# Attention times values: one more output store held back behind the last load, and SyncE's semaphore relays written as a register loop

## The chip, the cores and the metric

One core of one Trainium2 chip. The metric is the device time of one execution in microseconds (us), lower is better; medians of several executions are given. A profiled execution also has a *span*, from its first to its last instruction, which is about 2 us shorter than the device time. "Granted clock" is the share of full TensorE clock in the records. All runs below are of the fast state.

The engines by the names of the profile: PE (TensorE) makes the transposes and the products, DVE (VectorE) and ACT (ScalarE) copy their results, POOL (GpSimd) and SyncE (SP) issue transfers. A transfer is cut into packets, which the core's 16 DMA engines carry; it has *landed* when its semaphore says so.

## The reference

```python
def setup_inputs():
    batch, n_heads, seq, head_dim = 8, 12, 1024, 64
    ...                         # attn_weights (8,12,1024,1024), v (8,12,1024,64), float32
def reference(attn_weights, v):
    return np.einsum('bhqs,bhsd->bhqd', attn_weights, v).astype(np.float32)
```

403 MB of weights are read once, 25 MB of `v` are read and 25 MB of output are written. Heads are taken four at a time, in 24 groups (`NV = 24`); a group has two *units* of weights (`NU = 48`), each 8 MB of float32 in memory that become 4 MB of bfloat16 in SBUF.

## The kernel before: the parts that matter here

POOL issues all loads of weights and `v` and most stores. They stand in one ring, the software queue q0 of the profile. A load may be issued when PE has transposed the buffer that it overwrites. Group 0's `v` comes through SyncE.

```python
HELD = 6
HELD_FROM = NV - 1 - HELD          # 17
BY_SYNC = HELD_FROM + 3            # 20
BY_EIGHTS = HELD_FROM // 2         # 8: groups 0..15 use two output buffers in turn
NO = 2 + NV - 2 * BY_EIGHTS        # later groups have an output buffer each
...
for n in range(NU - 2):            # POOL
    pool.wait_ge(s_t[True], (n + 1) * PER_DVE)      # unit n is transposed
    load_attn(n + 2)
    if n % 2 == 0:
        q = n // 2
        ...                                          # wait for s_sp, then load_v(q + 1)
        if 0 < q <= HELD_FROM:
            store(q - 1)
for q in range(HELD_FROM, BY_SYNC):  # held stores 17, 18, 19: same ring, behind the last load
    store(q)
pool.drain()
```

The two units of the last group are loaded as halves (`s_second` is the second half's semaphore). SyncE passes on landings to the engines ("relays"), straight code for all 48 units. Then it stores groups 20 to 22 through its own ring (q1), then the last group in three pieces, and waits for all landings:

```python
for n in range(-2, NU - 2):
    if n + 2 < HALVED:
        nc.sync.wait_ge(s_abf[n % 2], 16 * ((n + 2) // 2 + 1))
    else:
        nc.sync.wait_ge(s_second[n + 2], 16)
    nc.sync.sem_inc(s_half)
    ...                                # every second n: s_v -> s_vr, landed store -> s_free
for q in range(BY_SYNC, NV - 1):
    store(q, by_sync=True)
...                                    # the last group: 512 KB, then 2 x 256 KB
for q in range(2 * BY_EIGHTS - 2, BY_SYNC):
    nc.sync.wait_ge(s_osb[slot(q)], ...)
nc.sync.wait_ge(s_end, 16 * (NV - 1 - BY_SYNC + 3))
```

Of the kernel before, what the change touches and what calls it, by code (L numbers as in the profile page):

```python
# [10 lines left out]
def kernel(  # L11
# [18 lines left out]
    nc = tc.nc  # L30
# [15 lines left out]
    NV = NH // VH  # L46
    NU = 2 * NV


    HELD = 6  # L50
    HELD_FROM = NV - 1 - HELD
    BY_SYNC = HELD_FROM + 3

    BY_EIGHTS = HELD_FROM // 2
    NO = 2 + NV - 2 * BY_EIGHTS

    HALVED = NU - 2

    def slot(q):
        return q % 2 if q < 2 * BY_EIGHTS else q - 2 * BY_EIGHTS + 2  # L60
# [15 lines left out]
    with tc.tile_critical(no_gpsimd_drain=True):  # L76
# [17 lines left out]
        s_abf = [sem(f"s_abf{i}") for i in range(2)]  # L94
        s_second = {n: sem(f"s_second{n}") for n in range(HALVED, NU)}
        s_v0, s_v = sem("s_v0"), sem("s_v")
        s_osb = [sem(f"s_osb{i}") for i in range(NO)]
# [13 lines left out]
        s_memset, s_const, s_vr = sem("s_memset"), sem("s_const"), sem("s_vr")  # L111

        s_half, s_free = sem("s_half"), sem("s_free")
# [206 lines left out]
        def store(q, by_sync=False):  # L320
            eng = nc.sync if by_sync else pool
            eng.wait_ge(s_out, 2 * q + 3)
            eng.dma_start(  # L323
                out=out_q[q],
                in_=osb[slot(q)].rearrange("p r d -> p (r d)"),
                **({} if by_sync else {"single_packet": True}),
            ).then_inc(s_end if by_sync else s_osb[slot(q)], 16)
# [9 lines left out]
            base=0,  # L337
# [4 lines left out]
        for h in range(VH):  # L342
# [6 lines left out]
                base=0,  # L349
# [3 lines left out]
        for n in range(NU - 2):  # L353
            pool.wait_ge(s_t[True], (n + 1) * PER_DVE)
# [3 lines that stand above are left out]
# [4 lines left out]
                if 0 < q <= HELD_FROM:  # L362
                    store(q - 1)
        for q in range(HELD_FROM, BY_SYNC):
            store(q)
# [2 lines left out]

        nc.sync.dma_start(out=v32.rearrange("p b x -> p (b x)"), in_=v_g[0]).then_inc(s_v0, 16)
        nc.sync.sem_inc(s_free, 2)  # L370
        for n in range(-2, NU - 2):

            if n + 2 < HALVED:
                nc.sync.wait_ge(s_abf[n % 2], 16 * ((n + 2) // 2 + 1))
            else:
                nc.sync.wait_ge(s_second[n + 2], 16)
            nc.sync.sem_inc(s_half)  # L377
            if n >= 0 and n % 2 == 0:
                q = n // 2
                nc.sync.wait_ge(s_v, 16 * (q + 1))  # L380
                nc.sync.sem_inc(s_vr)
                if 0 < q <= 2 * (BY_EIGHTS - 1):
                    nc.sync.wait_ge(s_osb[slot(q - 1)], 16 * ((q - 1) // 2 + 1))
                    nc.sync.sem_inc(s_free)
        for q in range(BY_SYNC, NV - 1):
            store(q, by_sync=True)
        rows = osb[slot(NV - 1)].rearrange("p (u half j) d -> p u half j d", u=2, half=2)
# [3 lines left out]
        for k in range(2):  # L391
            nc.sync.wait_ge(s_fin[k], 1)
            js = ds(4 * k, 4)
            nc.sync.dma_start(out=outs[:, 1, :, js], in_=rows[:, 1, :, js]).then_inc(s_end, 16)
        for q in range(2 * BY_EIGHTS - 2, BY_SYNC):
            nc.sync.wait_ge(s_osb[slot(q)], 16 * BY_EIGHTS if q < 2 * BY_EIGHTS else 16)
        nc.sync.wait_ge(s_end, 16 * (NV - 1 - BY_SYNC + 3))

# [29 lines left out]
```

## Time and profile before

| kernel before | |
|---|---|
| median on record before the change ran | 1055.79 us (1055.35 to 1056.08) |
| span of the profiled execution | 1053.9 us |
| busy share of PE / DVE / ACT | 71% / 37% / 38% |
| DMA engines' time filled by POOL's ring | 99.3% |
| last load landed | 1034.89 us |
| last copies of results done | 1048.54 us |

The reading begins with the row of the DMA engines and not with PE. The prediction shows the lines. One fact is not in any averaged view: the core's 16 DMA engines each have their own sequence of packets, and they do not finish together. So the tail of the run has to be read from the packet records.

### The profile page before, as it was taken

Reading aid. Unit: us, or ns where it says so; the run is one execution under the profiler, and the core shown is the slowest. Engines: PE = TensorE matmul, PEld = TensorE weight load, DVE = VectorE, ACT = ScalarE, POOL = GpSimd, SP = SyncE. Lnnn points to the kernel's source line nnn. Section 1 sums busy time; section 2 is a strip of 40 time slices with the busy share of each in tenths; the row PEclk is TensorE's granted clock in tenths of the full one; section 3 lists DMA queues with packets and bytes.
Section 4 is the critical chain, followed back from the end, with each engine's and each line's share of the span. In section 5 each row is a group of like instructions: output and inputs, shape, how many; then the busy total and the mean of one; then the engine's idle time right before and its main releaser. Section 6 shows DMA issues by size and latency. Waiting matters only on the chain.

```text
span 1053.9 us, 16410 instructions
## 1 busy us (share of the span) xinstructions
PE 752.7 (71%) x6920; PEld 707.1 (67%) x6920; DVE 388.1 (37%) x582; ACT 403.1 (38%) x489; POOL 52.4 (5%) x102
## 2 busy tenths in 40 slices
PE   0976686766878568776686767876678768776895
PEld 0866586756867568676676666765667758776784
DVE  1533343323433234332343333533334334433442
ACT  0543343433444334433353333433334334433452
POOL 1000000000000000000000000000000000000000
PEclk9989888888789888888888888988788898888897
DMA  9999999999999999999999999999999999999998
GB/s 220 219 219 207 239 230 219 238 210 246 238 218 233 209 240 238 218 238 214 243 238 214 236 220 229 238 219 238 234 222 231 219 211 218 218 219 218 211 218 314
DMA packets 14662, 239.67 MB, mean 227 GB/s; under 512 B 1600, under 2 KB 2112, under 8 KB 5184
## 3 DMA queue, kind: packets, MB, share of 16 engines
q0 software_dynamic: 13392, 234.36, 99.3%
q1 hardware_dynamic: 1264, 5.24, 1.2%
q8 instruction: 2, 0.03, 0.0%
q14 instruction: 4, 0.03, 0.0%
HBM read 427.82 MB, written 25.17 MB: 430 GB/s over the span
## 4 chain that ended last, share of the span: by engine, by line
DMA 76%; PE 22%; issue 1%; POOL 0%; DVE 0%; ACT 0%; SPq 0%; POOLq 0%
DMA abf<-in_attn_weights_dram 76%; PE bank L123 22%; PE bank L165 0%; PE bank L150 0%; POOL abf L310 0%; DVE osb L233 0%; ACT ot L262 0%; POOLq L423 0%; SPq L377 0%; SPq L76 0%
## 5 line engine op out<-in xcount | busy, mean ns | idle before, releaser
L123 PE MATMUL bank<-ident,abf 128*128 128x128 f32 x3072 | 468.7, 326 | 262.2 <-DMA abf<-in_attn_weights_dram 255.8
L123 PEld LDWEIGHTS bank<-ident,abf 128*128 128x128 f32 x3072 | 459.2, 215 | 275.1 <-DMA abf<-in_attn_weights_dram 268.3
L250 DVE COPY at<-bank 128x1024 bf16<-128x1024 bf16 x480 | 320.4, 689 | 495.0 <-PE bank L123 491.2
L250 ACT COPY at<-bank 128x1024 bf16<-128x1024 bf16 x288 | 289.1, 1012 | 428.2 <-PE bank L123 428.2
L165 PE MATMUL bank<-at,vbf 128*64 128x256 bf16 x3072 | 215.0, 278 | 0.0
L165 PEld LDWEIGHTS bank<-at,vbf 128*64 128x64 bf16 x3072 | 196.7, 108 | 13.4 <-DVE at L250 4.0
L262 ACT COPY ot<-bank 128x512 f32<-128x512 f32 x48 | 28.1, 585 | 181.1 <-PE bank L165 181.1
L262 DVE COPY ot<-bank 128x512 f32<-128x512 f32 x48 | 33.2, 692 | 151.4 <-PE bank L165 151.4
L150 PE MATMUL bank<-ident,ot 128*128 128x128 f32 x392 | 52.2, 276 | 33.0 <-DVE vbf L226 32.2
L150 PEld LDWEIGHTS bank<-ident,ot 128*128 128x128 f32 x392 | 43.4, 141 | 45.0 <-DVE vbf L226 44.0
L310 POOL DMA_DIRECT2D abf<-in_attn_weights_dram x50 | 26.6, 532 | 896.2 <-PE bank L123 895.2
L233 ACT COPY osb<-bank 128x512 f32<-128x512 f32 x97 | 52.1, 589 | 22.5 <-PE bank L150 22.5
L226 DVE CAST vbf<-bank 128x512 bf16<-128x512 f32 x48 | 30.9, 686 | 6.5 <-PE bank L138 6.5
L226 ACT CAST vbf<-bank 128x512 bf16<-128x512 f32 x48 | 25.8, 589 | 11.9 <-PE bank L138 11.9
L138 PE MATMUL bank<-vr,spread 32*128 32x512 bf16 x384 | 25.7, 377 | 0.0
L138 PEld LDWEIGHTS bank<-vr,spread 32*128 32x128 bf16 x384 | 9.9, 92 | 6.9
L316 POOL DMA_DIRECT2D vr<-in_v_dram x23 | 12.1, 528 | 19.2 <-PE bank L138 18.8
L323 POOL DMA_DIRECT2D out_dram<-osb x20 | 10.7, 537 | 37.3 <-ACT osb L233 37.3
L250 ACT ACT_TABLE_LOAD x8 | 10.3, 1283 | 1.2 <-SPq L76 1.1
L300 DVE CAST vr<-v 128x2048 bf16<-128x2048 f32 x1 | 1.4, 1403 | 3.3 <-DMA v<-in_v_dram 3.3
L344 POOL TENSOR_SCALAR_AFFINE_SELECT spread<-spread 32x512 bf16<-32x512 bf16 x4 | 2.5, 628 | 0.6
L233 DVE COPY osb<-bank 128x512 f32<-128x512 f32 x1 | 0.7, 692 | 3.1 <-PE bank L150 3.1
(8 smaller groups left out, 2.1 us busy)
## 6 DMA issues: line engine op xcount, KB each, us to landing
abf<-in_attn_weights_dram POOLq DMA_DIRECT2D x46, 4096.0 KB, 33.2
out_dram<-osb POOLq DMA_DIRECT2D x20, 1024.0 KB, 34.2
vr<-in_v_dram POOLq DMA_DIRECT2D x23, 512.0 KB, 34.2
abf<-in_attn_weights_dram POOLq DMA_DIRECT2D x4, 2048.0 KB, 25.8
out_dram<-osb SPq DMA_DIRECT2D x3, 1024.0 KB, 11.4
v<-in_v_dram SPq DMA_DIRECT2D x1, 1024.0 KB, 4.9
out_dram<-osb SPq DMA_DIRECT2D x1, 512.0 KB, 7.8
out_dram<-osb SPq DMA_DIRECT2D x2, 256.0 KB, 3.2
```

Source lines behind the costliest of these rows:

```text
L123: last = pe.matmul(out=pt[g % 4][:, k], lhsT=words[:, k], rhs=ident, is_transpose=True, start=(k == 0), stop=(k == KW - 1),)
L138: last = pe.matmul(out=ps, lhsT=spread[rows, b], rhs=vr[rows, b], start=(b == 0), stop=(b == VB - 1),)
L150: last = pe.matmul(out=ps[:, ds(j * P, P)], lhsT=ot[:, j0 + j], rhs=ident, is_transpose=True, start=(j == 0), stop=(j == jn - 1),)
L165: last = pe.matmul(out=outs, lhsT=vbf[:, 2 * kw + par, h], rhs=at[:, ds(half * GH, GH), kw, ds(h * VP, VP), par], start=(n == 0), stop=(n ...
L226: copy(out=vbf[:, :, h], in_=ps.rearrange("p (k d) -> p k d", k=SB)).then_inc(s_vbf[e])
L233: return copy(out=rows.rearrange("p (half j) d -> p j half d", half=2)[:, ds(j0, jn)], in_=ps[:, ds(0, jn * P)].rearrange("p (j half d) -> ...
L250: ins = copy(out=at[:, g].rearrange("c k j two -> c (k j two)"), in_=bank[g % 4].bitcast(bf16),)
L262: copy(out=ot.rearrange("c j (h p) -> c h j p", h=VH)[:, ds(2 * e, 2)], in_=po[e].rearrange("c (h j p) -> c h j p", h=2, j=GH),).then_inc( ...
L310: pool.dma_start(out=abf[n % 2][:, ds(g0, gn)].rearrange("p g s -> p (g s)"), in_=attn_q[n // 2][:, ds((n % 2 * G + g0) * S, gn * S)],).th ...
L316: pool.dma_start(out=vr.rearrange("p b x -> p (b x)"), in_=v_g[iv]).then_inc(s_v, 16)
L323: eng.dma_start(out=out_q[q], in_=osb[slot(q)].rearrange("p r d -> p (r d)"), **({} if by_sync else {"single_packet": True}),).then_inc(s_ ...
L344: pool.affine_select(out=spread[ds(h * VP, VP)], in_=spread[ds(h * VP, VP)], compare_op=mybir.AluOpType.not_equal, fill=1.0, base=0, patte ...
```

## The change

Its intent: hold seven stores instead of six, so that the last load comes earlier by one store, with the additional store in the ring of the loads; and shorten SyncE's instruction stream by a loop over eight heads (two groups) per pass.

```diff
-    HELD = 6
+    HELD = 7
     HELD_FROM = NV - 1 - HELD
-    BY_SYNC = HELD_FROM + 3
+    BY_SYNC = HELD_FROM + 4
...
-        for n in range(-2, NU - 2):
-            ...                     # waits and increments as above, straight
+        def relay(to, of, n):
+            nc.sync.wait_ge(of, n)
+            nc.sync.sem_inc(to)
+        ...
+        with nc.Fori(1, BY_EIGHTS, 1, engines=(mybir.EngineType.SP,)) as it:
+            base = nc.sync.snap(it * 32)
+            stored = nc.sync.snap(it * 16)
+            for k in range(2):
+                relay(s_half, s_abf[0], base + 16 * (k + 1))
+                relay(s_vr, s_v, base + 16 * k)
+                relay(s_free, s_osb[k], stored)
+                relay(s_half, s_abf[1], base + 16 * (k + 1))
+        for q in range(2 * BY_EIGHTS - 1, NV - 1):
+            relays_of(q)            # straight, as before
```

Group 16's store moves from the loop to behind the last load. `BY_EIGHTS` stays 8 and the number of output buffers stays 10.

> **What bounds the kernel now.** I read the page first: its busy shares, its DMA rows and its chain.
>
> ```profile
> PE 752.7 (71%) x6920; PEld 707.1 (67%) x6920; DVE 388.1 (37%) x582; ACT 403.1 (38%) x489; POOL 52.4 (5%) x102
> DMA  9999999999999999999999999999999999999998
> q0 software_dynamic: 13392, 234.36, 99.3%
> q1 hardware_dynamic: 1264, 5.24, 1.2%
> DMA 76%; PE 22%; issue 1%; POOL 0%; DVE 0%; ACT 0%; SPq 0%; POOLq 0%
> ```
>
> No compute engine is above 71%, the DMA engines are full in every slice, and the ring of POOL's transfers (q0) alone fills 99.3% of them. The 22% of PE in the chain are no evidence against that: a load may only be issued when PE has transposed the buffer it overwrites, so the chain runs through both. But a load of 4096 KB takes 33.2 us from issue to landing (the page's median) while one lasts about 20 us, so it stands in the ring some 13 us before the engines reach it. The limit is the sum of the bytes.
>
> Next, the chain in order of time, to see what one store costs inside the loop. The first five lines lie in iterations with a store, the next four without one (the kernel before stores its last one in the iteration at 786 to 829):
>
> ```profile
> 698.19 9.10 PE bank L123 x64
> ...
> 741.74 9.46 PE bank L123 x64
> ...
> 785.30 9.86 PE bank L123 x64
> ...
> 870.05 10.07 PE bank L123 x64
> ...
> 911.14 10.06 PE bank L123 x64
> ...
> 952.58 9.48 PE bank L123 x64
> ...
> 1003.96 30.91 DMA abf<-in_attn_weights_dram
> 1034.89 0.02 SPq L377
> 1034.95 5.75 PE bank L123 x32
> 1047.85 0.69 DVE osb L233
> ```
>
> Two units last 43.55 and 43.56 us with a store, 41.09 and 41.44 without (mean 41.27): a store of 1 MB in the ring costs about 2.3 us. The last load lands at 1034.9, and from there the remaining work on the last unit runs to 1048.5 before its last stores can go.
>
> Last, the stretches of that tail (columns: from:to, length, busy us of PE, PEld, DVE, ACT, POOL, granted clock, DMA share, GB/s):
>
> ```profile
> 1034.90:1038.00 3.10, 3.05 (x14) 3.05 (x15) 0.87 (x2) 1.01 (x1) 0.00 (x0) 0.50 1.01 428
> 1044.00:1046.00 2.00, 1.98 (x30) 1.66 (x27) 0.69 (x1) 0.00 (x0) 0.00 (x0) 1.00 1.02 430
> 1046.00:1048.00 2.00, 1.07 (x8) 0.86 (x8) 0.15 (x1) 1.17 (x2) 0.00 (x0) 1.00 0.95 395
> 1048.00:1049.00 1.00, 0.00 (x0) 0.00 (x0) 0.54 (x1) 0.00 (x0) 0.00 (x0) 1.00 0.40 162
> 1049.00:1050.00 1.00, 0.00 (x0) 0.00 (x0) 0.00 (x0) 0.00 (x0) 0.00 (x0) 0.56 1.01 350
> 1050.00:1051.00 1.00, 0.00 (x0) 0.00 (x0) 0.00 (x0) 0.00 (x0) 0.00 (x0) 0.50 0.62 214
> ```
>
> The six held stores keep the DMA full until about 1047.7. Only then is there a hole, 0.6 us wide on average in one microsecond, before the last unit's stores fill the engines again. That average hides what decides the case. The trace's packet records (start, duration, queue, size) chain end to start into 16 sequences, one for each DMA engine. They end their loads at different times, 1031.7 to 1034.5. The last one then has 24 packets of 8 KB from the ring of the loads and 24 from SyncE's, 0.307 us each (14.7 us, to 1049.3), 8 of 4 KB (1.25 us) and 32 of 1 KB (1.36 us): its last byte is at 1051.9, which is where the sequence does end, without a gap over 0.06 us. The span ends 2.0 us later. The engine that finishes last has no hole to be filled; the hole belongs to the engines that were ahead.
>
> **What the Trainium skill says.** "DMA: Bandwidth & Descriptors", section "Issuing engines are not separate DMA queues": transfers issued by different engines end up on the same 16 DMA engines and interleave. The trace agrees: in the tail both rings are at work and the rate stays at 428 to 430 GB/s, as with one. Its section "Queues, rings and completion order" has each engine take turns between the rings it has work for; so it matters little for the sum in which ring a store stands. Its section "Anatomy of one DMA" gives about 2.0 us of fixed cost, most of it the receipt after the last byte; here 1051.9 to 1053.9 fits. For the loop, "Advanced Engine Details and Errata", section "Control Flow Timing", gives 51 ns for a branch and 108 ns for compare-and-branch.
>
> **The change, part by part.**
> *The store moved.* HELD 6 to 7 moves the store of head group 16 from the loop to behind the last load, in the same ring; BY_SYNC stays 20, so SyncE's three stores are as before, and the number of osb buffers stays 10. Removed ahead of the last load: 8 packets of 8 KB on each DMA engine, 8 x 0.307 = 2.45 us, so the last load should land near 1032.4. Everything computed after it moves forward by as much: the last copies end near 1046.1 instead of 1048.5. Added after it: the same 2.45 us on each engine. For the slowest engine: 1034.5 - 2.45 = 1032.1, plus 56 packets x 0.307 = 17.2, plus 1.25 and 1.36, is 1051.9 again. What was gained before the landing is given back behind it: **0 us**. The engines that are ahead lose their hole of 0.5 to 0.9 us, which does not end the program sooner.
>
> *The relays in a loop.* SyncE waits for landings and raises s_half, s_vr and s_free. The order of these waits per iteration is the same as in the straight code, and the order of the other engines' instructions is unchanged but for the moved store. New is a little register arithmetic and one compare-and-branch for every two head groups, seven passes: with the skill's figure about 0.1 us each, plus the arithmetic. None of it is on the path: PE asks for s_half after half a unit of transposes, some 4 us after the landing of the same load, and SyncE's waits end with the DMA:
>
> ```profile
> SPq L377 <- DMA abf<-in_attn_weights_dram: 938.8, 48, 24.5
> SPq L381 <- DMA vr<-in_v_dram: 57.8, 23, 3.6
> ```
>
> The page's only waits of PE for SyncE (6.2 us) are with the halved loads of the end, which stay outside the loop. **0 us**.
>
> *Instruction words.* Fewer words of SyncE need fetching. In the span of the kernel before four packets of 8 KB of the instruction queue lie between the loads' (at 83, 427, 874 and 921 us), 0.3 us each on one engine; the one at 921 fell on an engine that was among the last. The trace does not tell which sequencer they fed. If one of the slowest engine's goes away, that is -0.3 us; I take about half: **-0.2 us**. If the loop fetched its words anew on each pass it would be plus, but PE runs 23 passes of its loop here and DVE 24, with only these four.
>
> Sum: 1055.8 - 0.2 = **1055.6 us**.
>
> **The rivals.** *The tail has room.* If the six stores ended before the last unit does, a seventh would be free and the gain 2.3 to 2.45 us, to 1053.4. For it: the mean share of 0.40 at 1048 to 1049 and the chain of waits, which ends in PE and DVE and not in the stores. Against it: the slowest engine's unbroken sequence. A part of it can come true if that engine is another one in other runs: with all engines level, the mean hole would be worth about 0.7 us.
> *The fuller ring delays the last stores.* The last unit's stores stand in SyncE's ring behind 3 MB and share the engines with 4 MB instead of 3 in the other. If the engines served the rings unevenly, they would land later, but only into time when the other ring is empty; the sum is the same. Small loss, below 0.5 us.
> *SyncE's loop becomes a wait.* Late relays would have to be over 4 us late to hold PE, and PE then some 10 us to starve the ring. To lose 2% (21 us) each of the seven passes would have to cost 3 us that nothing hides. I see no sign of it.
>
> **Range and chances.** The three runs before lie 0.7 us apart; which DMA engine is last, and by how much, depends on slow packets early in the run, so I allow about half a microsecond for that. Below, room for part of the first rival; above, for the second and some instruction fetches. 8 in 10: 1054.3 to 1056.5. Two per cent are 21 us, ten times more than the whole tail can hold: within 2% is 0.98.
>
> **What would show it.** Right: the chain's last load lands 2.2 to 2.6 us earlier, the last copies end as much earlier, and the stretch from the last load to the end of the span grows by as much (19.0 to about 21.4 us), with the DMA share near 1.0 until about 1049 and no dip to 0.4; SyncE's waits are still for DMA alone; the period of the iterations without a store stays at 41.3 us. Wrong: a span near 1051.5 with the tail still 19 us long (the tail had room, and the unbroken sequence was misread), or waits of PE or ACT for SyncE in the middle of the run, or more instruction packets (the loop costs).

## The result, and the profile after

1055.78 us median (1055.50 to 1056.49, 6 runs); the kernel before in the same rounds 1056.09 us (1055.35 to 1056.88, 6 runs). The ratio is 0.9998, 95% interval 0.9986 to 1.0011: the same. (Ratios are the mean time of one kernel's fast runs over that of the other's of the same rounds, so not quite the ratio of the medians.)

The page of the changed kernel answers with almost the same numbers; POOL's ring line is the same to the last digit. One line that differs is the instruction queue's, three packets instead of four:

```profile
q14 instruction: 3, 0.02, 0.0%
DMA 75%; PE 23%; issue 1%; POOL 0%; DVE 0%; ACT 0%; SPq 0%; POOLq 0%
```

The chain in order of time (start, duration, what). The iteration that lost its store is the one from 785 to 826:

```profile
741.84 10.01 PE bank L123 x64
...
785.40 10.32 PE bank L123 x64
...
826.50 10.29 PE bank L123 x64
...
1032.10 0.02 SPq L374
...
1032.16 6.03 PE bank L123 x32
...
1045.34 0.69 DVE osb L233
```

With its store, that iteration took 43.64 us in the kernel before (785.30 to 828.94); now it takes 41.10. The last load lands at 1032.10 instead of 1034.89, and the last copies are done at 1046.03 instead of 1048.54. Up to here the change gives what it was meant to give, 2.5 to 2.8 us. The span ends at 1053.6 instead of 1053.9. The tail from the last load to the end has grown from 19.0 to 21.5 us. The stretches of the tail (columns as in the prediction) show where the time went:

```profile
1044.00:1046.00 2.00, 1.06 (x8) 0.86 (x8) 0.66 (x1) 0.68 (x2) 0.00 (x0) 1.00 1.04 438
1046.00:1048.00 2.00, 0.00 (x0) 0.00 (x0) 0.04 (x1) 0.00 (x0) 0.00 (x0) 0.74 0.96 398
1048.00:1049.00 1.00, 0.00 (x0) 0.00 (x0) 0.00 (x0) 0.00 (x0) 0.00 (x0) 0.50 1.03 392
1049.00:1050.00 1.00, 0.00 (x0) 0.00 (x0) 0.00 (x0) 0.00 (x0) 0.00 (x0) 0.50 0.68 254
1050.00:1051.00 1.00, 0.00 (x0) 0.00 (x0) 0.00 (x0) 0.00 (x0) 0.00 (x0) 0.50 0.35 125
```

PE, DVE and ACT are done by 1046.1, and the DMA is still full until 1049. The dip to 0.40 that the kernel before had at 1048 to 1049 is gone, and the engines now stop one after another. The packet records name no DMA engine, so the prediction's chaining of them into 16 sequences is an inference, but their sizes and times alone bear its sum out. In the kernel before, only 5 packets are under way at 1048.75, and the last packet of 8 KB ends at 1049.26, of 4 KB at 1050.51 and of 1 KB at 1051.88 (the sum had 1049.3, 1050.5 and 1051.9). In the changed kernel all 16 engines are at work at 1048.75. The last group's stores tell the same from their side. In the page's issue list (size each, median us from issue to landing), first of the kernel before, then of the changed kernel:

```profile
out_dram<-osb SPq DMA_DIRECT2D x1, 512.0 KB, 7.8
out_dram<-osb SPq DMA_DIRECT2D x2, 256.0 KB, 3.2
```

```profile
out_dram<-osb SPq DMA_DIRECT2D x1, 512.0 KB, 9.6
out_dram<-osb SPq DMA_DIRECT2D x2, 256.0 KB, 5.2
```

They are issued 2.5 us sooner and take 1.8 to 2.0 us longer to land (medians).

### The profile page after: what moved, and what is told of

The parts are those of the page before. It is cut to its first block, busy times and chain, and to the rows that moved or that the text cites. A ratio compares the mean times of both kernels' runs of the same rounds, so it can differ in the third digit from the quotient of the medians.

```text
span 1053.6 us, 16446 instructions
## 1 busy us (share of the span) xinstructions
PE 755.9 (72%) x6920; PEld 710.4 (67%) x6920; DVE 388.5 (37%) x582; ACT 403.1 (38%) x489; POOL 52.4 (5%) x102
## 4 chain that ended last, share of the span: by engine, by line
DMA 75%; PE 23%; issue 1%; POOL 0%; DVE 0%; ACT 0%; SPq 0%; POOLq 0%
DMA abf<-in_attn_weights_dram 75%; PE bank L123 22%; PE bank L165 0%; PE bank L150 0%; POOL abf L310 0%; DVE osb L233 0%; ACT ot L262 0%; POOLq L435 0%; SPq L374 0%; SPq L76 0%
```

## The experiments

Two theories were set against each other, and a third came up on the way. **Full engines:** the DMA engine that ends last never idles, so a store costs it as much behind the last load as ahead of it. **Room in the tail:** the last unit's own work sets the end, a seventh held store is free, and something else, the loop, ate the gain. **Drain** is explained with the fifth experiment. By the 2% rule every one of the eleven runs is "the same" as the kernel before; what is read here are smaller differences. The 95% interval of the ratio leaves out 1 for three held (e4), nine held with six in the ring (e5), one store left out of seven (e6), e10 and e11, and for no other run.

**1 and 2. Each half of the change alone**

```diff
 # e1_held7_straight, from the kernel before
-    HELD = 6
+    HELD = 7
-    BY_SYNC = HELD_FROM + 3
+    BY_SYNC = HELD_FROM + 4
```
```diff
 # e2_held6_loop, from the changed kernel: the loop of relays stays
-    HELD = 7
+    HELD = 6
-    BY_SYNC = HELD_FROM + 4
+    BY_SYNC = HELD_FROM + 3
```

> The store move alone, SyncE's relays straight as before. Full engines (my theory: the DMA engine that ends last never idles, so the store costs as much behind the last load as ahead of it): 1055.8 us within 0.4, the last load landing near 1032.4 instead of 1034.9, four instruction packets as before. Rival 'room in the tail, and the loop ate the gain': 1053.4 us.

> The loop of relays alone, six stores held as before. Full engines: 1055.6 us within 0.5, last load at 1034.6 to 1034.9, three instruction packets instead of four. Rival 'the loop ate the gain': 1058 us, with the last load later than 1036.

Measured, beside 1055.54 us of the kernel before on the same chip: store move alone 1055.53 us (1055.47 to 1055.68, ratio 0.9999), loop alone 1055.73 us (1055.54 to 1056.30, ratio 1.0002). The last load landed at 1031.79 with the store moved and at 1034.43 with the loop alone (0.2 us sooner than I had expected). The store move alone gains nothing, and the loop alone loses nothing that could have hidden a gain: room in the tail falls. The instruction queue's line, first with the straight relays, then with the loop:

```profile
q14 instruction: 4, 0.03, 0.0%
```

```profile
q14 instruction: 3, 0.02, 0.0%
```

The packet that goes away is the one near 874 us. With six or seven stores held, straight relays have packets near 83, 427, 872 to 875 and 919 to 921 us, and the loop has none near 874. (With five and three held, where other engines' loops change too, the later packets lie at 853 and 1005 us, and at 833 us alone.) So the packet near 874 most likely fetched SyncE's words. The eighth experiment, which puts 160 instructions more into SyncE's loop, speaks for it: it has five packets, two of them new (137 and 1014 us). What it is worth, one packet of 0.32 us on one of 16 engines, is below what these runs can resolve.

**3 and 4. Fewer stores held**

```diff
 # e3_held5 and e4_held3, from the kernel before
-    HELD = 6
+    HELD = 5          # e4: 3
-    BY_SYNC = HELD_FROM + 3
+    BY_SYNC = HELD_FROM + 2          # e4: + 0
```

`BY_EIGHTS` follows `HELD` here: it becomes 9 and 10, so the number of output buffers falls to 8 and 6 and ACT's loop gets one and two passes more. These two runs change that as well.

> One store fewer held than before (5), straight relays. The last load lands 2.4 us later, near 1037.3. Full engines: at 5 the slowest engine gets its first gap, since the last unit's own work (about 13.6 us from landing to the last copies, 1.7 us more to its last packet, 2.0 us to the end) now ends after the stores: about +0.7 us, 1056.6. Rival 'room in the tail, the last unit's work sets the end at any count': +2.4 us, 1058.3.

> Three stores held, straight relays. Last load near 1042.2. Full engines: the stores end long before the last unit does, the end is the landing plus about 17.3 us: span 1059.5, +5.7 us, 1061.6. Rival 'last unit sets the end at any count': +7.3 us, 1063.2. A rival in which held stores are no use at all: 1055.8.

Measured: five held 1056.77 us (1056.57 to 1057.60, ratio 1.0013), three held 1061.57 us (1061.12 to 1062.31, ratio 1.0058). Both are within 0.2 us of what full engines expected. As steps from the kernel before it is less close: 1.2 and 6.0 us more were measured, where 0.7 and 5.7 were expected, and the interval of five held (0.9996 to 1.0030) still holds 1. With three held the tail has a real hole, as two of its stretches show: none of the DMA is busy while the last copies are made, then the last stores go alone.

```profile
1050.00:1053.00 3.00, 2.34 (x36) 2.01 (x32) 0.69 (x1) 0.59 (x1) 0.00 (x0) 1.00 0.44 173
1053.00:1055.00 2.00, 1.06 (x8) 0.86 (x8) 0.69 (x1) 0.59 (x1) 0.00 (x0) 1.00 0.00 0
```

Holding back stores is therefore worth its 2.4 us each as long as there is such a hole. From three held to five it gained 4.8 us, from five to six 1.2 us (medians of the same rounds; the second step is about the spread of the runs), and from six to seven nothing.

**5. More stores held**

```diff
 # e5_held9, from the changed kernel
-    HELD = 7
+    HELD = 9
-    BY_SYNC = HELD_FROM + 4
+    BY_SYNC = HELD_FROM + 6
-    BY_EIGHTS = HELD_FROM // 2
+    BY_EIGHTS = 8
```

> The changed kernel with nine stores held, six of them in the ring of the loads (the same number of buffers: the two stores more stay in the two buffers of the loop). The last load lands 4.8 us earlier than with seven, near 1027.3. Full engines: 1055.8 us within 0.4, the tail longer by 4.8 us. Rival 'room in the tail': 1051.

Measured: 1057.72 us (1057.40 to 1058.02) beside 1055.58, ratio 1.0019, interval 1.0002 to 1.0036. It is well below 2%, but neither theory expected it: the slowest run of the kernel before in these rounds took 1056.05. The last load landed at 1027.02, as expected, and by the packet records the last packet of all ended at 1051.37, no later than with seven held (1051.60). So the DMA was done and the program was not. SyncE's list of waits has a line that no kernel so far had:

```profile
SPq L76 <- POOLq L76: 2.2, 1, 2.2
```

SyncE, with all stores landed, waits 2.2 us for POOL. POOL's last instruction of its own is `pool.drain()`. In the trace it begins when POOL has issued its stores and goes on until some time after their last packet; it ends here at 1054.35, which is 4.2 us after the last packet of POOL's ring (1050.17). In all ten traces at hand at that point (a text below says eleven, a miscount) the drain ended 4.1 to 4.2 us after that packet. This is the third theory, "drain": nine held with six in POOL's ring was slow because that ring ended too late for its drain.

**6 and 7. One store of the tail left out**

```diff
 # e6_drop_of7 from the changed kernel, e7_drop_of6 from the kernel before; wrong on purpose
-        for q in range(HELD_FROM, BY_SYNC):
+        for q in range(HELD_FROM, BY_SYNC - 1):
             store(q)
...
-        for q in range(2 * BY_EIGHTS - 2, BY_SYNC):
+        for q in range(2 * BY_EIGHTS - 2, BY_SYNC - 1):
```

> The changed kernel with the last store of the loads' ring left out (wrong on purpose: head group 19 is not written). Full engines: every engine has 8 packets of 8 KB less in the tail, 2.45 us, and nothing else sets the end: 1053.4 us. Rival 'the last unit's compute sets the end': no change, 1055.8.

> The kernel before with the same store left out (wrong on purpose: head group 19 is not written). Full engines: the slowest engine would be done 2.45 us sooner, but the last unit's last packets come only near 1050.3, so 1.6 us are gained, 1054.3: less than with seven held. Rival 'the last unit's compute sets the end': no change, 1055.9.

Measured: from the changed kernel 1053.10 us (1052.93 to 1053.35), ratio to the kernel before 0.9976, interval 0.9959 to 0.9992, so 2.5 us less. Out of seven, a store left out gives back its whole cost: the tail of the changed kernel is set by the DMA. From the kernel before 1055.42 us (1054.46 to 1055.77), ratio 0.9994, where I had expected 1054.3: a partial miss. Its profiled execution was the slowest of the four. Two pieces of its chain, and a stretch of its tail:

```profile
1035.00 6.70 PE bank L123 x32
1048.85 0.69 DVE osb L233
```

```profile
1047.00:1050.00 3.00, 1.06 (x8) 0.86 (x8) 0.69 (x1) 1.17 (x2) 0.00 (x0) 1.00 0.04 16
```

The 32 transposes after the last load, which begin after a wait of 5.6 us at a granted clock of 0.5, took 6.70 us here and 5.75 in the kernel before. (The granted clock of the stretch from 1038 to 1041 is 0.50 here and 0.85 there.) By the packet records no packet at all moved from 1048.1 to 1049.9, and all final packets came late, ending together at 1051.5. My expectation had taken the faster transposes, and 1.7 us from the last copies to the last packet where 2.0 were measured (1049.54 to 1051.58). With one store less the last unit's work sets the end; with six stores both are within some tenths of each other.

**8. Relays made late**

```diff
 # e8_late, from the changed kernel
         def relay(to, of, n, late=0):
             nc.sync.wait_ge(of, n)
+            for _ in range(late):
+                nc.sync.sem_inc(s_idle)
             nc.sync.sem_inc(to)
...                                     # in the loop, both relays to s_half:
-                relay(s_half, s_abf[0], base + 16 * (k + 1))
+                relay(s_half, s_abf[0], base + 16 * (k + 1), 40)
```

> The changed kernel with 40 idle semaphore increments ahead of each of the loop's raises of s_half, which make these relays some us later in all seven passes. Full engines: hidden, 1055.8 us within 0.4. Rival 'the relays are on the path': about +2 us for each of 28 relays, 1110; if only a part shows, PE waits for SyncE in the middle of the run.

Measured: 1055.69 us (1055.31 to 1056.42), ratio 1.0001. By the trace one such relay came 2.5 us after the landing (305.73 to 308.26). The waits of PE for SyncE are unchanged, and both belong to the halved loads of the end, outside the loop:

```profile
PE bank L123 <- SPq L378: 6.2, 2, 5.6
```

Relays 2.5 us late in every pass still cost nothing. In the changed kernel the end of one pass, from the register addition to the last register instruction of the next, takes 0.29 us (175.66 to 175.94), and SyncE has some 19 us until the next landing.

**9 to 11. The drain**

```diff
 # e9_held9_four_in_ring, from e5_held9: four in POOL's ring, five by SyncE
-    BY_SYNC = HELD_FROM + 6
+    BY_SYNC = HELD_FROM + 4
```
```diff
 # e10_held7_six_in_ring, from the changed kernel: six in POOL's ring, one by SyncE
-    BY_SYNC = HELD_FROM + 4
+    BY_SYNC = HELD_FROM + 6
```
```diff
 # e11_held9_no_drain, from e5_held9
-        pool.drain()
```

> Nine stores held, four of them in POOL's ring and five by SyncE. Theory 'drain': nine held with six in the ring was slower because POOL's drain ends 4.2 us after the last packet of its ring (it does so in all eleven traces), and six stores make that ring end too late; with four the ring ends early enough, so 1055.8 us within 0.5, drain over before SyncE's last wait. Rival 'number held' (the tail loses something with each further store): 1057.7 as with six in the ring.

> Seven stores held, six of them in POOL's ring and one by SyncE. Theory 'drain': the ring's last packet comes near 1051, the drain ends near 1055.3 and the span 1.15 us later: 1058.7 us. Rival 'number held': 1055.8 as with four in the ring.

> Nine stores held, six in the ring, POOL's own drain after its last store taken out (SyncE still waits for every store's landing). Theory 'drain': 1055.8 us within 0.5. If the closing drains of the program wait as long as this one did: 1057.7.

Measured, beside 1055.63: nine held with four in the ring 1055.61 us (1055.47 to 1055.79, ratio 0.9999); seven held with six in the ring 1057.62 us (1057.49 to 1058.14, ratio 1.0019), and its SyncE waits for POOL as well:

```profile
SPq L76 <- POOLq L76: 2.3, 1, 2.3
```

Not the number held but the number in POOL's ring makes the difference. Seven held with six in the ring came out 1.1 us below what was expected for it: its ring ended at 1050.0 and not near 1051. Without the drain, nine held took 1063.03 us (1062.72 to 1063.72, ratio 1.0072), worse than either side expected. The program ends with a drain on POOL of its own. In the other twelve kernels it took 0.05 us; here it began at 1051.82, after the ring was long done (1049.91), and took 7.65 us. Why it takes that long, and longer than the 4.2 us of the early one, no run shows. What they do show is that a drain issued early does its waiting beside the transfers.

The numbers that decide, all from the traces' packet and instruction records (us from the start of the span):

| kernel | last packet, POOL's ring | POOL's drain ends | last packet of all | SyncE's last wait over | span |
|---|---|---|---|---|---|
| before (3 in the ring) | 1045.58 | 1049.75 | 1051.88 | 1052.22 | 1053.9 |
| changed (4) | 1047.76 | 1051.93 | 1051.60 | 1051.94 | 1053.6 |
| e1, store alone (4) | 1047.41 | 1051.61 | 1051.26 | 1051.61 | 1053.3 |
| e2, loop alone (3) | 1045.12 | 1049.30 | 1051.42 | 1051.77 | 1053.4 |
| e4, three held (0) | 1041.25 | 1045.37 | 1056.95 | 1057.30 | 1058.9 |
| e6, seven less one (3) | 1042.65 | 1046.81 | 1048.95 | 1049.30 | 1050.9 |
| e5, nine held (6) | 1050.17 | 1054.35 | 1051.37 | 1051.73 | 1055.5 |
| e9, nine held (4) | 1042.80 | 1046.90 | 1051.55 | 1051.91 | 1053.5 |
| e10, seven held (6) | 1050.00 | 1054.28 | 1051.16 | 1051.52 | 1055.5 |

The fourth column is the plainest evidence for full engines. With six, seven or nine stores held, in whichever ring, the last packet ends between 1051.1 and 1051.9 (e8 and e11, not in the table, at 1051.41 and 1051.11). It moves when work is taken away from seven (e6) and when too little is held (e4, and e3 with 1052.35). It does not move when the same store is taken away from six (e7, 1051.58), since there the last unit's own work takes over. In three of the thirteen traces all 16 DMA engines stand idle before the last stores, for 0.9 us in e3, 3.8 in e4 and 1.8 in e7. In the kernel before, the changed one and the others they never do.

## Why the prediction was right or wrong

The prediction was 1055.6 us (8 in 10: 1054.3 to 1056.5), 0.2 us less than before; measured were 1055.78, 0.3 us less than the kernel before in the same rounds. "No change" is what held; that the figure came so close is luck, since differences of 0.2 to 0.3 us are well inside the spread of either kernel's runs.

- **The store moved, 0 us.** Right, and shown: the store move alone is 0.9999 of the kernel before, and leaving one store out of seven gives back 2.5 us. The cost of 2.45 us before the landing is borne out by the iteration that lost its store (43.64 to 41.10) and by the landing, 2.79 us sooner in this pair of traces, a little outside the 2.2 to 2.6 that the prediction named as the sign. The excess over 2.45 is of the size of one instruction packet, but other pairs show no such rule (3.1 us between the kernel before and e1, 2.3 between e2 and the changed kernel). A likely reason is the engines' spread at the last load, which differs from run to run: 2.1 to 2.9 us in these four.
- **The relays in a loop, 0 us.** Right: the loop alone measured 1.0002, and 2.5 us of added delay stays hidden. The iterations without a store kept their period (41.06 to 41.15 us in the changed kernel), and SyncE's waits in the loop are for DMA alone.
- **Instruction words, -0.2 us.** The mechanism fits: one packet goes away, most likely SyncE's. Its worth in time is not settled; six runs of one kernel spread over 1.0 to 1.5 us.
- **The wait that ends the program.** Here the prediction misread the tail. It put the 2.0 us from the last byte to the end of the span down to the receipt of the last byte, with a figure that the page gives for transfers issued by POOL; the last stores are SyncE's. In the trace SyncE's last wait is over 0.34 us after the last packet (1051.88 to 1052.22). The other 1.6 us are the program's closing instructions. The sum was the same, so the number did not suffer.
- **"The fuller ring delays the last stores", below 0.5 us.** The size holds for four stores. But its reason, that the sum of packets alone decides, lacks POOL's drain, which ends 4.2 us after the ring. In the changed kernel the drain and SyncE's last wait end within 0.01 us of each other (1051.93 and 1051.94): four stores are about the most that ring can hold here without cost, and six cost 2.0 us (five were not run). The packet records show both rings' packets side by side in the tail, but as they name no DMA engine, no run shows that one engine takes turns between the rings.
- **"The tail has room", 1053.4 us.** Refuted by e1, e2 and e6. The shadow of truth in it is the knee: up to five stores held there is room, at six almost none.
- **Two readings of the page.** "Full in every slice" is not quite what the DMA row says: its last slice, the tail, has 8 of 10. And "428 to 430 GB/s, as with one" ring has to be set beside the page's 430 GB/s of bytes read and written in HBM over the span. The rate column of the stretches shows only 218 to 221 while loads run, since a load of 8 MB counts there with the 4 MB that it writes.

None of the versions tried that compute the right result is faster than the kernel before by more than the spread of its runs. With the DMA engines filled from the first load to the last store, only less work for them made the time shorter in these experiments (e6, 2.5 us).

## What to carry to other kernels

Moving a transfer off the path to the last load pays only as long as the engines would otherwise stand idle behind it; find the knee by the transfer engine that ends last, not by the average share. When the tail was full (six to nine held here), the count of held stores no longer mattered, but the ring they stood in did: a closing drain that follows its own ring by some us (4.2 here) must have its ring finished early, and it should be issued early. Relays that an engine asks for later than they come can be rewritten for short code at no cost.

## What the Trainium skill lacked or had wrong

- "DMA: Bandwidth & Descriptors", section "Anatomy of one DMA", puts about 2.0 us of fixed cost on a transfer that POOL issues, most of it the receipt. The receipt is much shorter here: the last packet of POOL's ring in the kernel before ends at 1045.58 and its last semaphore increment comes at 1045.91, 0.33 us later, with the DMA engines full. For SyncE's final stores, another path, it is 0.34 us from the last packet to the end of the wait, and 0.9 us from the issue (1048.03) to the first packet on engines that stood idle (1048.93).
- No page gives the cost of POOL's drain behind a busy ring: 4.1 to 4.3 us after the ring's last packet when issued early (twelve traces, the one without the drain left out), and 7.65 us when it began only after the ring had been done for 1.9 us. "VectorE: DVE Perf Modes", section "The DRAIN you can't avoid", says of the drains around a program that they are about 12 ns, constant; the first of POOL's at the end took 47 ns in the other kernels and 7.65 us in e11.
- No page gives a size for how far apart 16 equally loaded DMA engines end: 2.1 to 2.9 us at the last load here (four traces), which is what an averaged DMA share hides.
- "Advanced Engine Details and Errata", section "Control Flow Timing": its 51 and 108 ns are for single branches. From the start of the loop's compare-and-branch to SyncE's next instruction the changed kernel took 0.17 us (175.73 to 175.90); the whole end of a pass, with its register arithmetic, took 0.29 us.
